# Tying normalised rows and turned residual blocks behind the next block's weight split in a hybrid attention layer

## The chip, the cores and the metric

The kernel runs on one core of one Trainium2 chip, in one launch. The metric is the device time in microseconds of that core, as the median of several runs: 1050.98 us here (three runs, 1050.15 to 1051.49). The core has five engines that each work through a queue of their own in order: TensorE (PE for its matmuls, PEld for the weight loads that go ahead of them), VectorE (DVE), ScalarE (ACT), GpSimd (POOL) and SyncE (SP, which here only issues DMAs). An instruction that waits for a semaphore holds up everything behind it in its engine's queue.

## The reference, cut to what matters

One post-norm decoder layer: 256 tokens and 16 meta tokens of width 2048, all in float32.

```python
p = h @ w_in                                  # q heads, shared latent, indexer, pool channels
# group A: an indexer scores the keys, each query keeps its top 64, attention over the latent
# group B: trailing means over 2, 4, 8, 16 tokens minus the token, a map per group
mix = concat(A, B) @ w_o
h = layer_norm(ALPHA * h + mix, ln1_g, ln1_b)
z = causal_conv3(h @ w_up)                    # to 2 * 5632 channels
a, g = split(z)
f = (gelu(a) * g) @ w_down
h = layer_norm(ALPHA * h + f, ln2_g, ln2_b)
return h[:, N_META:]
```

The indexer's score of a key is `sum_h w[t,h] * relu(q_idx[t,h] . k_idx[s])`. The two layer norms need a mean and a variance over the 2048 channels of a token.

## The kernel before, in words

**Number format.** A float32 product is made from three matmuls of a reduced format. Every operand is split into an upper part, rounded by an ACT copy, and a lower part, which is what DVE has left after subtracting the upper part. For weights this is `fetch` (L109 to L125): one DMA of a 128x2048 block into a `wraw` buffer (L110), then for each half of the block an ACT copy (L123) and a DVE subtraction (L124) into `whl`. `product` (L189 to L197) runs three matmuls for each of the 16 tiles of the contraction: upper by upper (L195), upper by lower (L196), lower by upper (L197). So one block of weights with 258 columns of activations is 48 matmuls, and its first L197 needs the DVE half of the first split.

**Order of weights.** All weight blocks stand in one list, `stream`. `weights` (L161) hands out the next block and first calls `emit` for the blocks up to two ahead. There are three `wraw` and three `whl` buffers. `state["use"]` is the number of the next block that will be handed out, and `split[i]` keeps the last ACT and the last DVE instruction of block i's split.

**Order of instructions.** The kernel is traced in program order, and a scheduler then orders each engine's queue by what it reckons to be ready first, so an instruction can be issued much earlier than it is written, or later. `behind(i)` (L168) lays down an order: whatever is traced inside it is queued, if it runs on ACT, after the last ACT instruction of block i's split, and if it runs on DVE, after the last DVE instruction of it. It adds no wait for completion, and it leaves PE, POOL and SP alone. Before the change only `forms` is traced inside it.

**The stages.** In order of time: indexer queries (8 blocks) with `dots` (L346, scores of two indexer heads on PE, relus on ACT, sums on DVE), the `w_uk` block whose eight products are copied by ACT to `kt` (L395), with the dots of the last query block traced after the copy of h == 2; values, top-64 selection on DVE, query heads, attention and pooling; the output projection (16 blocks, `output`), which also makes sums and sums of squares over the channels on POOL (L629 to L633); then the feed-forward part (88 up blocks, `up f half`, with w_down blocks between them from f = 8 on).

**Around the change.** The first four pairs of up blocks (f < 4, eight blocks, FOLDED = 4) run on activations that are not normalised yet (`folded`). Their results are corrected afterwards by `unfold` (L712 to L720: DVE copy L715, DVE multiply L717, ACT L719, POOL add L720), followed by the convolution `conv` (ACT L707, DVE L708 and L709) and `gate` (ACT L724, DVE L725). The column sums over the channels that the first layer norm needs, `deviation` (L662, matmuls of a column of ones in `column_sums`, L242) and `deviation_rows` (L677), are traced inside the first of these blocks, after its tiles 7 and 14. While these eight blocks run, `normalise(m)` prepares the 16 normalised activations for f >= 4: POOL multiply (L689), DVE add (L690), ACT scale and shift (L691), ACT upper part (L693), DVE lower part (L694); three of them are traced behind each block until all 16 are made. After the pairs f = 4 and f = 5 eight DVE transposes each (L870) turn the 32x32 squares of the normalised rows in place, and from f = 6 to f = 11 `residual` (L701) moves them with 32 DMAs on ACT's queue into `y2`, the sum that the w_down products are added to. Every one of these DMAs reads all 16 turned tiles. PSUM is two pools of four banks: `big()` for the weight products, `small()` for the rest, `kt` and `dots` among it.

Of the kernel before, what the change touches and what calls it, by code (L numbers as in the profile page):

```python
# [17 lines left out]
P = 128  # L18
D = 2048
NM = 16  # L20
# [4 lines left out]
KT = D // P  # L25
# [11 lines left out]
FOLDED = 4  # L37
MF = 80 + C
NE = NQ + 2
# [28 lines left out]
def tile_layer(ctx, tc, xt, w_first, w_proj, w_uk, w_uv, w_pool, w_o, w_up, w_down, cols, rows, rel_bias, onehot, out):  # L68
    nc = tc.nc
# [7 lines left out]
    def big():  # L77
        return pm.tile([P, 512], F32, tag="mm", name="mm")

    def small():  # L80
        return pa.tile([P, 512], F32, tag="at", name="at")
# [4 lines left out]
    ps = small()  # L86
# [20 lines left out]
    state = {"next": 0, "use": 0}  # L107
# [53 lines left out]
    def weights(ahead=2):  # L161
        i = state["use"]
        state["use"] += 1
        prefetch(i + 1 + ahead)
        return ready.pop(i)

    @contextmanager
    def behind(i):  # L168

        upper, lower = (getattr(ins, "ins", ins) for ins in split[i])  # L170
        with tc.issue_after(upper), tc.issue_after(lower):
            yield
# [8 lines left out]
    def row_sums(i, hl):  # L181

        total = sb.tile([P, 1], F32, name=f"total{i}")
        nc.scalar.activation(raws[i], raws[i], AF.Copy, accum_out=total)
        hi, lo = (hl[-1][:, p, 256:] if isinstance(hl, list) else hl[:, p, 2048:] for p in range(2))
        nc.scalar.activation(hi, total.to_broadcast([P, 2]), AF.Copy)
        nc.vector.tensor_tensor(lo, total.to_broadcast([P, 2]), hi.bitcast(F32), op=ALU.subtract)

    def product(ps, hl, m, act, lo, hi, ks=range(KT), width=P, k0=0, k1=KT):  # L189

        for n in range(k0, k1):
            k = ks[n]
            wh, wl = hl[:, 0, k * width:k * width + m], hl[:, 1, k * width:k * width + m]
            ah, al = act[k][:, 0, lo:hi], act[k][:, 1, lo:hi]
            nc.tensor.matmul(ps, wh, ah, start=n == 0, stop=False)  # L195
            nc.tensor.matmul(ps, wh, al, start=False, stop=False)  # L196
            nc.tensor.matmul(ps, wl, ah, start=False, stop=n == KT - 1)  # L197
# [6 lines left out]
    for k0, k1 in [(k, k + 1) for k in range(9)] + [(9, 12), (12, 15), (15, 16)]:  # L204
# [6 lines left out]
        if k0 % 6 == 0:  # L211
            hl = wp.tile([P, 2, 2048 + 2], F32R, tag="whl", name="whl")
# [22 lines left out]
    def col(base, j):  # L235
        return cv[:, base + j:base + j + 1]
# [25 lines left out]
    ps = heads[0][0]  # L262
# [22 lines left out]
    for j in range(2):  # L285
        ps = heads[1 + j][0]
# [5 lines left out]
    ps = small()  # L292
# [53 lines left out]
    def dots(j, qi, pa_, heads):  # L346

        for i in heads:
            h = 2 * j + i
            pb = small()  # L350
            for o, n, t in ((pa_[:, S * i:S * i + S], S, slice(0, P)), (pb[:, :T], T, slice(P, S))):
                nc.tensor.matmul(o, qi[:, i, t], kidx[:, 0, :n], start=True, stop=False)
                nc.tensor.matmul(o, qi[:, i, t], kidx[:, 1 + i, :n], start=False, stop=True)
            rl = temp([P, KW], "rl")
            nc.scalar.activation(rl[:, :KA], pa_[:, S * i:S * i + KA], AF.Relu)
            nc.scalar.activation(rl[:, KA:], pb[:, :T], AF.Relu)
            for i2, (a, b) in enumerate(((0, KA), (KA, KW))):
                nc.vector.scalar_tensor_tensor(score[:, a:b], rl[:, a:b], widx[:, i2, h:h + 1], score[:, a:b],
                                               op0=ALU.mult, op1=ALU.add)
# [3 lines left out]
    for j in range(8):  # L363
        hl = weights()
        ps = big()
# [22 lines left out]
    for h in range(H):  # L388
        ps = small()
        for c in range(2):  # L390
            w = slice(1024 * c + h * HD, 1024 * c + h * HD + HD)
            nc.tensor.matmul(ps[:, :T], uk[:, 0, w], ctp[:, c, 0, :], start=c == 0, stop=False)
            nc.tensor.matmul(ps[:, :T], uk[:, 0, w], ctp[:, c, 1, :], start=False, stop=False)
            nc.tensor.matmul(ps[:, :T], uk[:, 1, w], ctp[:, c, 0, :], start=False, stop=c == 1)
        nc.scalar.activation(kt[:, h, :], ps[:, :T], AF.Copy)  # L395
        if h == 2:
            dots(7, qis[7], small(), (0, 1))

    y = sb.tile([P, KT, T], F32, tag="y", name="x", padded_shape=[P, KT, T])
# [3 lines left out]
    for i, (a, b) in enumerate(((0, NM), (NM, NM + P), (NM + P, T))):  # L403
# [6 lines left out]
        for g in range(2):  # L410
            ps = small()
# [27 lines left out]
    for h in range(H):  # L439
        hl = weights()  # L440
        ps = big()
# [5 lines left out]
    ps = small()  # L447
# [120 lines left out]
    for h in range(H):  # L568
# [3 lines left out]
        hl = weights()  # L572
        ps = big()
# [46 lines left out]
    folded = []  # L620
# [22 lines left out]
    for m in range(1, KT):  # L643
# [5 lines left out]
        if m == KC:  # L649
            ps = small()  # L650
# [34 lines left out]
    h_parts = []  # L685

    def normalise(m):
        yd = y[:, m, Q0:]
        nc.gpsimd.tensor_tensor(yd, yd, rs, op=ALU.mult)  # L689
        nc.vector.tensor_tensor(yd, yd, m2, op=ALU.add)  # L690
        nc.scalar.activation(yd, yd, AF.Identity, bias=col(LN1, 2 * m + 1), scale=col(LN1, 2 * m))  # L691
        a = ring.tile([P, 2, T], F32R, tag="act", name="hp")
        nc.scalar.activation(a[:, 0, :NQ], yd, AF.Copy)  # L693
        nc.vector.tensor_tensor(a[:, 1, :NQ], yd, a[:, 0, :NQ].bitcast(F32), op=ALU.subtract)  # L694
        h_parts.append(a)
# [108 lines left out]
    for item in plan:  # L804
        if item[0] in "AB":
            seven(*item)
            continue
        if item[0] == "down":
            _, part, c, g = item
            hl = weights()  # L810
            if c == 1:
                emit((last, spare)[g])
                if g == 0:
                    row_sums(last, ready[last])
            if g == 0:
                downs = [big(), big()]
            n = PARTS[part]
            for k in range(4 * g, 4 * g + 4):
                w = slice(512 * (k - 4 * g), 512 * (k - 4 * g) + 512)
                for i in range(2):  # L820
                    a, r = pairs[part][k // 2][f"a{i + 1}{k % 2 + 1}"]
                    nc.tensor.matmul(downs[i], a[:, 0, r], hl[:, 0, w], start=k == 0, stop=False)
                    nc.tensor.matmul(downs[i], a[:, 0, r], hl[:, 1, w], start=False, stop=False)
                    nc.tensor.matmul(downs[i], a[:, 1, r], hl[:, 0, w], start=False, stop=k == n - 1)
            if g == n // 4 - 1:
                for i in range(2):
                    yc = y2[:, i, 512 * c:512 * c + 512]
                    nc.vector.tensor_tensor(yc, yc, downs[i], op=ALU.add)
            continue
        _, f, half_ = item  # L830
        part = next(p for p in range(len(PARTS)) if f < sum(PARTS[:p + 1]))
        if half_ == 0:
            if f % 2 == 0:
                pair = fp.tile([P, 2, S], F32, name="za", tag="z0", bufs=3)
            both = []
        hl = weights()
        ps = big()
        if todo and f > FOLDED + half_:
            p, r = todo.pop(0)
            with behind(state["use"]):  # L840
                pairs[p].append(forms(r, len(pairs[p]), p == FAST))
        if f < FOLDED:
            k = 0
            if f + half_ == 0:
                product(ps[:, :NE], hl, P, folded, 0, NE, k1=7)
                deviation()
                product(ps[:, :NE], hl, P, folded, 0, NE, k0=7, k1=14)
                deviation_rows()
                k = 14
            product(ps[:, :NE], hl, P, folded, 0, NE, k0=k)  # L850
            while len(h_parts) < min(KT, 3 * (2 * f + half_ + 1)):
                normalise(len(h_parts))
            both.append(ps)
            if half_ == 0:
                continue
            both = [conv(i * FT + f, i, unfold(both[i]), pair[:, f % 2]) for i in range(2)]
        else:
            product(ps[:, :NQ], hl, P, h_parts, 0, NQ)
            both.append(conv(half_ * FT + f, half_, ps, pair[:, f % 2]))
            if half_ == 0:  # L860
                continue
        gate(*both)
        if part > FAST:
            a = fp.tile([P, 2, NE], F32R, name="gp", tag="gp", bufs=16)
            gated.append(two_parts(a[:, :, :S], both[0]))
        elif f % 2:
            todo.append((part, pair))
        if f in (FOLDED, FOLDED + 1):
            for m in range(8 * (f - FOLDED), 8 * (f - FOLDED) + 8):
                nc.vector.transpose(y[:, m, NM:], y[:, m, NM:])  # L870
        if FOLDED + 2 <= f < FOLDED + 8:
            for _ in range((6, 5, 5)[f % 3]):
                residual(*moves.pop(0))
# [57 lines left out]
    for i in range(2):  # L931
        t, mv = slice(i * P, (i + 1) * P), mvs[i]
        waiting = []
        for q, (a, b) in enumerate(cuts[i]):
            ps = small() if i else big()
# [91 lines left out]
```

## Time and profile before

| what | value |
|---|---|
| time, median of 3 runs | 1050.98 us (1050.15 to 1051.49) |
| profiled execution, its own time | 1050.0 us |
| span of that execution (first to last instruction) | 1048.2 us |
| mean granted TensorE clock | 0.998 |
| PE busy / PEld busy | 99% / 94% of the span |
| DVE busy | 85%, 890.0 us |
| ACT busy | 59%, 621.3 us |
| POOL busy | 20%, 212.4 us |
| HBM read | 232.50 MB, 224 GB/s over the span |

Busy shares are over the whole span. A matmul's recorded duration is longer than the distance to the next one (they are pipelined), so short losses of PE show in the distance between starts, not in its busy share. In a view of waits, a line names the engine and line that waited, the engine and line that ended the wait, the total in us, the number of waits and the longest.

### The profile page before, as it was taken

How to read it: one execution, taken by the hardware profiler on the slowest of the kernel's cores; microseconds unless marked ns; L12 is line 12 of the kernel's file. 1: busy time of each engine (PE TensorE's matmuls, PEld its weight loads, DVE VectorE, ACT ScalarE, POOL GpSimd, SP SyncE). 2: the span in 40 equal slices, each digit the busy share in tenths (PEclk: the TensorE clock that was granted, in tenths of full speed). 3: DMA queues.
4: the chain of work that ended last, by engine and by line, in shares of the span. 5: the costliest groups of instructions: out<-in, count | busy, mean ns of one | idle time of the engine just before them, and what ended most of it. 6: DMA issues, size and time to landing. Idle time of an engine off the chain costs nothing. (4 is left out here: it accounts for less than half of the span.)

```text
span 1048.2 us, 19242 instructions
## 1 busy us (share of the span) xinstructions
PE 1035.8 (99%) x7671; PEld 986.4 (94%) x7671; DVE 890.0 (85%) x1381; ACT 621.3 (59%) x998; POOL 212.4 (20%) x264
## 2 busy tenths in 40 slices
PE   9999999999999999999999999999999999999996
PEld 8998999999999999999999999999999999999985
DVE  6879468858879997898989989898898899989876
ACT  7566346745447765566556655566655666555674
POOL 1100014125436231102112011120211212220030
PEclk9999999999999999999999999999999999999999
DMA  8756542454552577898887787887878778787773
GB/s 324 256 172 241 185 153 97 143 194 162 197 191 92 198 228 226 274 297 275 270 289 277 277 279 267 286 275 266 285 271 288 273 284 275 266 285 270 290 224 128
DMA packets 59322, 249.75 MB, mean 238 GB/s; under 512 B 21686, under 2 KB 22112, under 8 KB 32224
## 3 DMA queue, kind: packets, MB, share of 16 engines
q1 hardware_dynamic: 34160, 229.76, 60.3%
q0 software_dynamic: 7600, 15.62, 7.8%
q10 hardware_dynamic: 17472, 3.15, 1.7%
q8 instruction: 60, 0.98, 0.4%
q14 instruction: 30, 0.25, 0.1%
HBM read 232.50 MB, written 2.11 MB: 224 GB/s over the span
## 5 line engine op out<-in xcount | busy, mean ns | idle before, releaser
L124 DVE TENSOR_TENSOR whl<-wraw,whl 128x1024 fp32r<-128x1024 f32 (+1 forms) x416 | 489.5, 1212 | 43.3 <-ACT whl L123 42.6
L123 ACT ACTIVATE whl<-wraw 128x1024 fp32r<-128x1024 f32 (+1 forms) x416 | 402.5, 1015 | 114.8 <-DVE wraw L119 28.5
L196 PE MATMUL mm<-hp,whl 128*128 128x258 f32 x1280 | 362.4, 283 | 0.0
L195 PE MATMUL mm<-hp,whl 128*128 128x258 f32 x1280 | 361.9, 283 | 0.0
L197 PE MATMUL mm<-hp,whl 128*128 128x258 f32 x1280 | 361.0, 282 | 0.0
L195 PEld LDWEIGHTS mm<-hp,whl 128*128 128x128 f32 x1280 | 242.4, 189 | 3.2
L196 PEld LDWEIGHTS mm<-hp,whl 128*128 128x128 f32 x1280 | 242.5, 189 | 3.1
L197 PEld LDWEIGHTS mm<-hp,whl 128*128 128x128 f32 x1280 | 242.9, 190 | 0.0
L195 PE MATMUL mm<-xp,whl 128*128 128x256 f32 (+5 forms) x384 | 111.8, 291 | 0.0
L196 PE MATMUL mm<-xp,whl 128*128 128x256 f32 (+5 forms) x384 | 108.9, 284 | 0.0
L197 PE MATMUL mm<-xp,whl 128*128 128x256 f32 (+5 forms) x384 | 108.7, 283 | 0.0
L707 ACT ACTIVATE z<-mm,cv 128x256 f32<-128x256 f32 x40 | 22.6, 565 | 93.9 <-PE mm L197 93.5
L196 PEld LDWEIGHTS mm<-xp,whl 128*128 128x128 f32 x384 | 72.3, 188 | 0.8 <-issue 0.5
L195 PEld LDWEIGHTS mm<-xp,whl 128*128 128x128 f32 x384 | 72.4, 189 | 0.6
L197 PEld LDWEIGHTS mm<-xp,whl 128*128 128x128 f32 x384 | 72.4, 189 | 0.3 <-DVE whl L124 0.2
L773 PE MATMUL at<-whl,gp 128*128 128x512 f32 x180 | 71.2, 395 | 0.0
L774 PE MATMUL at<-whl,gp 128*128 128x512 f32 x180 | 71.1, 395 | 0.0
L772 PE MATMUL at<-whl,gp 128*128 128x512 f32 x180 | 71.1, 395 | 0.0
L747 POOL TENSOR_TENSOR forms<-za 128x128 f32<-128x128 f32 x20 | 24.8, 1239 | 220.6 <-DVE za L725 214.9
L707 ACT ACTIVATE za<-mm,cv 128x256 f32<-128x256 f32 x40 | 22.6, 565 | 62.5 <-PE mm L197 61.7
L744 POOL TENSOR_TENSOR forms<-za 128x128 f32<-128x128 f32 x20 | 22.2, 1112 | 121.3 <-DVE za L725 117.2
L115 DVE TENSOR_TENSOR wraw<-wraw 128x512 f32<-128x512 f32 x36 | 24.7, 685 | 19.8 <-DMA wraw<-in_w_down 19.8
(327 smaller groups left out, 1950.1 us busy)
## 6 DMA issues: line engine op xcount, KB each, us to landing
wraw<-in_w_up SPq DMA_DIRECT2D x88, 1024.0 KB, 5.1
wraw<-in_w_down SPq DMA_DIRECT2D x80, 1024.0 KB, 6.2
wraw<-in_w_proj SPq DMA_DIRECT2D x24, 1024.0 KB, 5.0
wraw<-in_w_o SPq DMA_DIRECT2D x16, 1024.0 KB, 4.9
y<-v POOLq DMA_DIRECT2D x27, 256.0 KB, 8.7
y<-u POOLq DMA_DIRECT2D x18, 256.0 KB, 4.7
wraw<-in_w_first SPq DMA_DIRECT2D x8, 304.0 KB, 5.2
x<-in_xt SPq DMA_DIRECT2D x1, 2176.0 KB, 8.6
```

What stands on the lines that cost most here:

```text
L115: nc.vector.tensor_tensor(b12, b12, b11, op=ALU.subtract)
L123: upper = nc.scalar.activation(hl[:, 0, c], raw[:, c], AF.Copy)
L124: lower = nc.vector.tensor_tensor(hl[:, 1, c], raw[:, c], hl[:, 0, c].bitcast(F32), op=ALU.subtract)
L195: nc.tensor.matmul(ps, wh, ah, start=n == 0, stop=False)
L196: nc.tensor.matmul(ps, wh, al, start=False, stop=False)
L197: nc.tensor.matmul(ps, wl, ah, start=False, stop=n == KT - 1)
L707: nc.scalar.activation(z, src[:, 2:NQ], AF.Identity, bias=col(C_B, j), scale=col(C_W, 3 * j + 2))
L744: nc.gpsimd.tensor_tensor(s[:, 0], a21, a22, op=ALU.add)
L747: nc.gpsimd.tensor_tensor(s[:, 3], a11, a21, op=ALU.subtract)
L772: nc.tensor.matmul(ps, a[:, 0, i], hl[:, 0, w], start=j == 0, stop=False)
L773: nc.tensor.matmul(ps, a[:, 0, i], hl[:, 1, w], start=False, stop=False)
L774: nc.tensor.matmul(ps, a[:, 1, i], hl[:, 0, w], start=False, stop=j == n - 1)
```

## The change

Four edits.

1. The dots of the last query block are traced after the `kt` copy of h == 3, not of h == 2.
2. In the first up block, `deviation` comes after 8 tiles, not 7, and `deviation_rows` after 15, not 14.
3. `normalise` is traced inside `behind(state["use"])`: its ACT and DVE instructions are queued after the split of the block that is handed out next. Its POOL multiply is not tied.
4. The transposes are traced after the pairs f = 3 and f = 4, not 4 and 5, and inside `behind(state["use"])`.

```diff
         nc.scalar.activation(kt[:, h, :], ps[:, :T], AF.Copy)
-        if h == 2:
+        if h == 3:
             dots(7, qis[7], small(), (0, 1))
...
             if f + half_ == 0:
-                product(ps[:, :NE], hl, P, folded, 0, NE, k1=7)
+                product(ps[:, :NE], hl, P, folded, 0, NE, k1=8)
                 deviation()
-                product(ps[:, :NE], hl, P, folded, 0, NE, k0=7, k1=14)
+                product(ps[:, :NE], hl, P, folded, 0, NE, k0=8, k1=15)
                 deviation_rows()
-                k = 14
+                k = 15
             product(ps[:, :NE], hl, P, folded, 0, NE, k0=k)
-            while len(h_parts) < min(KT, 3 * (2 * f + half_ + 1)):
-                normalise(len(h_parts))
+            with behind(state["use"]):
+                while len(h_parts) < min(KT, 3 * (2 * f + half_ + 1)):
+                    normalise(len(h_parts))
...
-        if f in (FOLDED, FOLDED + 1):
-            for m in range(8 * (f - FOLDED), 8 * (f - FOLDED) + 8):
-                nc.vector.transpose(y[:, m, NM:], y[:, m, NM:])
+        if FOLDED - 1 <= f <= FOLDED:
+            with behind(state["use"]):
+                for m in range(8 * (f - FOLDED + 1), 8 * (f - FOLDED + 1) + 8):
+                    nc.vector.transpose(y[:, m, NM:], y[:, m, NM:])
```

## The prediction

> **What bounds the kernel now.** I read the busy shares first, then the waits of the weight loads, then busy time by stretch, and last the timelines around each wait.
>
> ```profile
> span 1048.2 us, 19242 instructions
> PE 1035.8 (99%) x7671; PEld 986.4 (94%) x7671; DVE 890.0 (85%) x1381; ACT 621.3 (59%) x998; POOL 212.4 (20%) x264
> ```
> ```profile
> PEld at L554 <- ACT df L546: 1.1, 1, 1.1
> PEld mm L197 <- DVE whl L124: 1.1, 3, 0.6
> ...
> PEld at L242 <- POOL sums L633: 0.4, 1, 0.4
> PEld at L352 <- ACT kt L395: 0.4, 1, 0.4
> ```
> ```profile
> 316.00:330.00 14.00, 14.00 (x120) 14.00 (x119) 14.00 (x22) 9.05 (x18) 13.28 (x15) 1.00 0.21 76
> ...
> 350.00:360.00 10.00, 9.93 (x83) 9.72 (x82) 10.00 (x19) 8.04 (x13) 2.71 (x2) 1.00 0.57 190
> 400.00:600.00 200.00, 200.00 (x1432) 188.88 (x1431) 178.71 (x246) 117.80 (x165) 30.88 (x36) 1.00 0.83 275
> ```
>
> The columns of the last fence are stretch, length, and busy us of PE, PEld, DVE, ACT and POOL, then granted clock, DMA share and GB/s. TensorE sets the end: it is busy 99% of the span, and in 400 to 600 us it never idles. So a change that adds no matmul can gain only what TensorE waits for. Of its waits, three lines of four are touched by the four edits: L352 (dots), L242 (column sums), L197 behind the splits. Beside these waits stands DVE, full in both the earlier stretches (14.00 of 14, 10.00 of 10): there the order of its queue decides which block's split comes late.
>
> **The change part by part.** A matmul of 258 or 260 columns follows the one before after 0.12 us, as 338.75 and 338.87 do in the second fence below; what a wait costs is the distance beyond that.
>
> *Dots.* PE first, then ACT.
> ```profile
> 81.69 0.28 PE L196 MATMUL mm<-xp,whl 128*128 128x258 f32 x1
> 81.99 0.39 PE L197 MATMUL mm<-xp,whl 128*128 128x258 f32 x1
> 82.22 0.28 PE L195 MATMUL mm<-xp,whl 128*128 128x258 f32 x1
> 82.64 0.39 PE L352 MATMUL at<-kidx,qi 128*128 128x272 f32 x1
> ...
> 81.11 1.06 ACT L123 ACTIVATE whl<-wraw 128x1024 fp32r<-128x1024 f32 x1
> 82.19 0.97 ACT L395 ACTIVATE kt<-at 128x272 f32<-128x272 f32 x3
> ```
> PE loses 0.18 us to 81.99, 0.11 us to 82.22 and 0.30 us to 82.64: 0.59 us. The second dots bank is the one that kt 0 leaves, and ACT copies it only after a split, at 82.19. One more kt product (six matmuls, 0.75 us) now goes ahead, but then all four banks are taken by kt, so the first dots bank too waits for the first copy, near 82.59. PE would get there at 81.34 + 0.75 = 82.09 and wait 0.5 us, unless the scheduler fills in query matmuls as at 81.69. Gain 0.59 at best, loss 0.1 at worst (a restart like 82.22's); I take 0.3, as both rows of filler and of copy lie near. Moved with it are 8 matmuls, 4 relus and 4 DVE sums, no DMA; the top-64 search behind them starts up to 0.75 us later, which the eight query blocks on PE (48 matmuls of 0.12 us each, 46 us) hide; without that cover it would cost the same 0.75 us.
>
> *Column sums.*
> ```profile
> 309.71 0.86 PE L242 MATMUL at<-ones,sums 128*128 128x64 f32 x6 [0.24 <-POOL sums L633]
> L633 POOL TENSOR_TENSOR sums<-sums,sq x1: 1627/1627/1627, 308.0 to 308.0; 128x258 f32<-128x258 f32 x1
> ```
> The squares are ready at 308.03 + 1.63 = 309.66. One more tile is three matmuls, 0.36 us, longer than the idle 0.24 us, so the wait goes, and perhaps the 0.11 us restart: 0 to 0.35, I take 0.3. Twelve matmuls of `deviation_rows` move by the same tile; they were not waiting. No queue of DMAs is passed.
>
> *Ties.* Two up blocks waited, PE first, then DVE, then ACT:
> ```profile
> 338.75 0.28 PE L195 MATMUL mm<-fold,whl 128*128 128x260 f32 x1
> 338.87 0.28 PE L196 MATMUL mm<-fold,whl 128*128 128x260 f32 x1
> 339.55 0.39 PE L197 MATMUL mm<-fold,whl 128*128 128x260 f32 x1 [0.40 <-DVE whl L124]
> 339.77 0.28 PE L195 MATMUL mm<-fold,whl 128*128 128x260 f32 x1
> ...
> 351.05 0.28 PE L196 MATMUL mm<-fold,whl 128*128 128x260 f32 x1
> 351.40 0.39 PE L197 MATMUL mm<-fold,whl 128*128 128x260 f32 x1
> ```
> ```profile
> 336.25 0.75 DVE L690 TENSOR_TENSOR x<-x,of_token 128x258 f32<-128x258 f32 x2
> ...
> 337.60 0.75 DVE L690 TENSOR_TENSOR x<-x,of_token 128x258 f32<-128x258 f32 x2
> 338.28 2.35 DVE L124 TENSOR_TENSOR whl<-wraw,whl 128x1024 fp32r<-128x1024 f32 x2
> ...
> 343.37 1.18 DVE L124 TENSOR_TENSOR whl<-wraw,whl 128x1024 fp32r<-128x1024 f32 x1
> ...
> 349.81 0.43 DVE L870 STREAM_TRANSPOSE x<-x 128x256 f32<-128x256 f32 x1
> 350.16 2.32 DVE L124 TENSOR_TENSOR whl<-wraw,whl 128x1024 fp32r<-128x1024 f32 x2
> 352.40 0.98 DVE L694 TENSOR_TENSOR hp<-x,hp 128x258 fp32r<-128x258 f32 x1
> ```
> ```profile
> 337.00 2.00 ACT L123 ACTIVATE whl<-wraw 128x1024 fp32r<-128x1024 f32 x2
> 348.42 2.00 ACT L123 ACTIVATE whl<-wraw 128x1024 fp32r<-128x1024 f32 x2
> ```
> The first wait costs 339.55 - 338.87 - 0.12 = 0.56 and a restart of 0.10, together 0.66 us; the second 0.35 - 0.12 = 0.23 and as much restart, 0.33 us. Counting the L690 from their first, the four at 336.25 and 337.60 are rows 12 to 15. Traced behind block up-2-0 (f = 2, first half) and the one after it, they are now tied behind the split at 338.28 or the next: 1.5 us leave the front of it. But ACT writes its first half only at 337.00 + 1.05 = 338.05, and what stands before that on ACT are rows 6 to 8, tied to a split long done. So DVE can start 338.28 - 338.05 = 0.23 us earlier and no more: gain 0.23, bounds 0 and 0.66. At the second wait ACT is done at 349.47 and DVE starts at 350.16, behind a transpose that is now tied behind a split after it.
> ```profile
> L870 DVE STREAM_TRANSPOSE x<-x x16: 396/431/436, 341.6 to 367.2; 128x256 f32<-128x256 f32 x16
> ```
> Five transposes from 341.6 to 349.81, some 0.35 us of DVE each (349.81 to 350.16), leave; the four L690 (1.5 us) come in. The 0.35 us in front of the split goes, and with the 0.23 from above the start is 349.5 to 349.6, the end 0.6 us earlier; 0.23 is needed. Gain 0.33, bounds 0 and 0.33.
>
> What is late next? Everything moved is wanted late: the last L694 ends at 353.4, and the first block that reads it begins three blocks (144 matmuls, 17.3 us) before 374.30, at 357.0, and needs its sixteenth tile 45 matmuls on, at 362.4, so 9 us cover the rows; if they used that up, each us more would be a us of PE. The transposes feed only the 32 DMAs on ACT's queue.
>
> **The sum.** 0.3 + 0.3 + 0.23 + 0.33 = 1.16 us off the profiled execution, 1050.0 (a span of 1048.2 and 1.8 us around it): 1048.8. The median lies 0.98 above that run, so 1049.8. All bounds at their best: 0.59 + 0.35 + 0.66 + 0.33 = 1.93 us, 1049.0; all at their worst, 0.1 slower, 1051.1.
>
> **The rivals.**
>
> *The ties don't bind.* On ACT no L691 or L693 stood in front of the split it is now tied behind, and the splits' ACT halves set their time. If the DVE order hardly changes, both block waits stay and only 0.6 us is gained: 1050.4. For it speaks the 0.23 us above; against it the five DVE items in front of the splits.
>
> *ACT's queue stops at the residual DMAs: slower.*
> ```profile
> 367.20 0.43 DVE L870 STREAM_TRANSPOSE x<-x 128x256 f32<-128x256 f32 x1
> 367.56 1.41 DVE L124 TENSOR_TENSOR whl<-wraw,whl 128x1024 fp32r<-128x1024 f32 x1
> ...
> 367.92 1.40 ACTq L701 DMA_DIRECT2D y<-x  x2
> 369.84 2.01 ACT L123 ACTIVATE whl<-wraw 128x1024 fp32r<-128x1024 f32 x2
> ...
> 371.60 2.35 DVE L124 TENSOR_TENSOR whl<-wraw,whl 128x1024 fp32r<-128x1024 f32 x2
> 374.30 0.28 PE L195 MATMUL mm<-hp,whl 128*128 128x258 f32 x1
> ```
> Before, the first DMA is issued 0.3 us after the last transpose. Transposes 8 to 15 now stand behind the split that ends at 368.97. Between that and the next split at 371.60 lie 2.6 us of other DVE work; with half of it and eight transposes of 0.35 us, the last ends at 368.97 + 1.3 + 2.8 = 373.1 and not 367.6, and an L701 that keeps its place holds ACT 5.5 us longer. Behind it on ACT is the split of the block that PE begins at 374.30; its DVE half is done at 371.60 + 1.2 = 372.8, needed two matmuls in, at 374.54, and has 1.7 us to spare. So PE loses 3.8 us, net 2.6 slower: 1053.6. It decides from a last transpose after 367.6 + 1.7 = 369.3. Against it: DVE, rid of the early transposes, reaches that split sooner, and the scheduler can put the DMAs further back, as what they move is wanted only many blocks later.
>
> *Contention moves the wait to the next block.*
> ```profile
> L690 DVE TENSOR_TENSOR x<-x,of_token x16: 415/460/965, 315.5 to 337.9; 128x258 f32<-128x258 f32 x16
> ```
> An L690 follows the next after 0.37 us at 336.25, but takes up to 0.965 beside POOL's multiplies. The four moved ones now meet two POOL adds of `unfold` before the split at 343.37: 1.5 + 2 x 0.6 - 1.05 (three transposes gone) = 1.65 us later, where the next block, which PE begins 45 matmuls after 339.77, at 345.16, has its split at 344.55 and wants it at 345.40, 0.85 us to spare: 0.8 us back, 1050.6. The Trainium skill (SBUF — State Buffer, Who interferes with whom) says that a DVE instruction with two SBUF inputs and a GpSimd instruction that reads SBUF exclude one another, whichever starts first; the spread of L690 agrees. By that rule the transposes, with one input, cost POOL nothing.
>
> *More than the touched waits.* A new order from the dots on also removes the L554 wait of 1.1 us, with all of the 1.93: 3.0 us, 1048.0. Only the scheduler's freedom speaks for it.
>
> **How the numbers follow.** Forecast 0.50, ties idle 0.10, contention 0.08, ACT's queue 0.14, more 0.18. Of the forecast's own spread, 1049.0 to 1050.6, a median of three that scatters by 0.7 us takes a tenth beyond 2.1 us; 0.2%, 2.1 us, is about what a measurement of this kernel can tell from no change. Faster: 0.18 and 0.06 of the forecast, 0.24. Slower: 0.14 and 0.02, 0.16. Same: 0.60. The range goes from 1048.2, near the case of more, to 1052.4, halfway into the case of ACT's queue (a stall of 2.5 us); the forecast alone gives 1049.0 to 1050.6.
>
> **What would show it.** PE's wait at L242 gone; at L352 smaller; L197's total of 1.1 us down to some 0.4; L690 12 to 15 after the split near 338; no L870 before 355; the last L870 near 369 to 372. A PE wait near 374 with ACT held at L701 would prove the slower case; PE waits in stretches that have none now would make the forecast wrong altogether.

## The result, and the profile after

| what | before | after |
|---|---|---|
| time, median of 6 runs each | 1050.61 us (1049.91 to 1051.49) | 1055.04 us (1052.90 to 1057.46) |
| ratio to before | | 1.004, 95% interval 1.003 to 1.005 |
| profiled execution, its own time | 1050.0 us | 1057.46 us |
| its span | 1048.2 us | 1055.7 us |

The change makes the kernel 4.4 us slower; 1049.8 was forecast. The profiled execution of after is the slowest of its six runs, 2.4 us over the median, so its sizes are upper ones. The head of its page and its waits of the weight loads:

```profile
span 1055.7 us, 19243 instructions
PE 1037.3 (98%) x7671; PEld 987.4 (94%) x7671; DVE 889.9 (84%) x1381; ACT 621.0 (59%) x998; POOL 211.9 (20%) x264
```
```profile
PEld at L773 <- DVE whl L124: 5.4, 1, 5.4
...
PEld at L554 <- ACT df L546: 1.1, 1, 1.1
...
PEld at L352 <- ACT kt L395: 0.6, 1, 0.6
```

The busy shares hardly differ from before, DVE's work is the same 890 us, and ACT's is 621. The list of waits differs: L242 behind the column sums is gone, and so is L197 behind the splits, all 1.1 us of it. In their place stands one wait, 5.4 us, at a line (L773, a product of the w_down blocks) that did not wait at all before. To see where it lies, the start of the same matmul in both traces (numbers count the core's 7671 matmuls from 0):

| matmul | before, us | after, us | after - before |
|---|---|---|---|
| 2600 | 327.12 | 326.88 | -0.24 |
| 2700 | 339.77 | 338.87 | -0.90 |
| 3000 | 376.10 | 375.04 | -1.06 |
| 3600 | 455.59 | 454.52 | -1.07 |
| 4000 | 512.08 | 518.68 | +6.60 |
| 7300 | 974.42 | 981.01 | +6.59 |
| 7670 (the last) | 1038.58 | 1045.55 | +6.97 |

So of the forecast gain of 1.16 us nearly all arrived, 1.06 us by 376 us, and was kept for 80 us. Then 7.7 us were lost in one place between 455 and 519 us, and kept to the end. Of the other 0.9 us of the span, 0.4 lie between 981 us and the last matmul and 0.5 behind it; no edit touches these. The place itself, in after's timelines of PE, DVE and SP:

```profile
457.78 0.40 PE L772 MATMUL at<-whl,right 128*128 128x512 f32 x1
463.28 0.79 PE L773 MATMUL at<-whl,right 128*128 128x512 f32 x1 [5.11 <-DVE whl L124]
463.88 0.63 PE L774 MATMUL at<-whl,right 128*128 128x512 f32 x1
```
```profile
452.60 0.69 DVE L118 TENSOR_TENSOR wraw<-wraw 128x512 f32<-128x512 f32 x1 [0.74 <-DMA wraw<-in_w_down]
...
455.70 0.43 DVE L725 TENSOR_TENSOR za<-za,z 128x256 f32<-128x256 f32 x1
461.40 0.69 DVE L118 TENSOR_TENSOR wraw<-wraw 128x512 f32<-128x512 f32 x1 [5.28 <-DMA wraw<-in_w_down]
462.01 4.09 DVE L124 TENSOR_TENSOR whl<-wraw,whl 128x1024 fp32r<-128x1024 f32 x4
```
```profile
449.62 0.33 SPq L110 DMA_DIRECT2D wraw<-in_w_up  x1
451.89 0.33 SPq L110 DMA_DIRECT2D wraw<-in_w_down  x1
```

Three weight blocks matter. By their place in `stream` they are numbers 71 (w_down), 72 (up) and 73 (w_down). A w_down block of this kind is first folded in its `wraw` buffer by three DVE instructions (L118 to L120 of `fetch`) and then split as any block is (L123 on ACT, L124 on DVE); another kind has one such instruction, L115. The row at 452.60 is the fold of block 71. PE begins block 71 at 457.78 and needs its lower half for the second matmul. DVE had nothing to do from 456.1 on, but the next row in its queue was the fold of block 73, whose transfer was issued only at 451.89 and landed at 461.4, 9.5 us later. The four L124 behind it are the lower halves of blocks 71 and 72. ACT had made the upper halves of block 71 by 455.97, so its split was ready during the whole wait; those of block 72, whose transfer landed at 458.0, were made by 460.1. Before, at the same place, the order was the other one:

```profile
454.14 0.69 DVE L120 TENSOR_TENSOR wraw<-wraw 128x512 f32<-128x512 f32 x1
...
455.66 1.22 DVE L124 TENSOR_TENSOR whl<-wraw,whl 128x1024 fp32r<-128x1024 f32 x1
456.79 0.42 DVE L725 TENSOR_TENSOR za<-za,z 128x256 f32<-128x256 f32 x1
457.13 3.22 DVE L124 TENSOR_TENSOR whl<-wraw,whl 128x512 fp32r<-128x512 f32 x3
460.28 0.68 DVE L118 TENSOR_TENSOR wraw<-wraw 128x512 f32<-128x512 f32 x1
```

There the splits of 71 and 72 stand ahead of the fold of 73, which comes at 460.28 and waits for nothing. So the loss was a row of DVE's queue that waits for a DMA ahead of rows that are ready. The Trainium skill (TensorE: Matmul & The Clock Gate, Architectural detail) calls the queues of ACT and DVE strict first-in, first-out; the 5.28 us in which DVE idled with block 71's split ready behind the fold agree.

What led up to it shows in the groups of the transposes and of the residual DMAs, after (L872 is L870 of before):

```profile
L872 DVE STREAM_TRANSPOSE x<-x x16: 397/430/439, 357.0 to 374.7; 128x256 f32<-128x256 f32 x16
```
```profile
L701 ACTq DMA_DIRECT2D y<-x x32: 592/602/3017, 375.2 to 474.1; - x32
```

The figures are shortest, median and longest ns, then first and last start. Before, the transposes ran from 341.6 to 367.2 and the DMAs were issued from 367.9 to 464.0:

```profile
L701 ACTq DMA_DIRECT2D y<-x x32: 592/626/1987, 367.9 to 464.0; - x32
```

The tie has put the last transpose 7.5 us later and the first DMA 7.3 us. Of the 10.1 us by which the last DMA is later, most is not a cause of the loss but its result: in the run e2 below, which keeps all ties and has no stall near 460, the last DMA is issued at 466.4, 2.4 us later than before.

### The profile page after: what moved, and what is told of

The parts are those of the page before. It is cut to its first block, busy times and chain, and to the rows that moved or that the text cites. A ratio compares the mean times of both kernels' runs of the same rounds, so it can differ in the third digit from the quotient of the medians.

```text
span 1055.7 us, 19243 instructions
## 1 busy us (share of the span) xinstructions
PE 1037.3 (98%) x7671; PEld 987.4 (94%) x7671; DVE 889.9 (84%) x1381; ACT 621.0 (59%) x998; POOL 211.9 (20%) x264
## 5 line engine op out<-in xcount | busy, mean ns | idle before, releaser
L124 DVE TENSOR_TENSOR whl<-wraw,whl 128x1024 fp32r<-128x1024 f32 (+1 forms) x416 | 489.7, 1212 | 46.3 <-ACT whl L123 45.5
L123 ACT ACTIVATE whl<-wraw 128x1024 fp32r<-128x1024 f32 (+1 forms) x416 | 402.9, 1015 | 133.2 <-DVE wraw L119 32.3
L197 PE MATMUL mm<-hp,whl 128*128 128x258 f32 x1280 | 361.3, 282 | 0.0
L197 PEld LDWEIGHTS mm<-hp,whl 128*128 128x128 f32 x1280 | 243.1, 190 | 0.0
L197 PE MATMUL mm<-xp,whl 128*128 128x256 f32 (+5 forms) x384 | 108.6, 283 | 0.0
L197 PEld LDWEIGHTS mm<-xp,whl 128*128 128x128 f32 x384 | 72.4, 189 | 0.0
L773 PE MATMUL at<-whl,gp 128*128 128x512 f32 x180 | 71.4, 397 | 0.0
L115 DVE TENSOR_TENSOR wraw<-wraw 128x512 f32<-128x512 f32 x36 | 24.7, 686 | 20.4 <-DMA wraw<-in_w_down 20.4
```

Source lines behind the costliest of these rows:

```text
L115: nc.vector.tensor_tensor(b12, b12, b11, op=ALU.subtract)
L123: upper = nc.scalar.activation(hl[:, 0, c], raw[:, c], AF.Copy)
L124: lower = nc.vector.tensor_tensor(hl[:, 1, c], raw[:, c], hl[:, 0, c].bitcast(F32), op=ALU.subtract)
L773: nc.tensor.matmul(ps, a[:, 0, i], hl[:, 1, w], start=False, stop=False)
```

## The experiments

Theory A: the loss is the order on DVE alone, the fold of block 73 ahead of the splits of 71 and 72; the tie of the transposes (edit 4) makes this order, and the other edits are harmless. Rival R1: the residual DMAs, which now come later on ACT's queue, cost the time by themselves, by holding ACT or by slowing the weight transfers. Rival R2: the earlier start of everything behind 339 us, or the tie of the normalised rows, is to blame. Line numbers in the traces of the experiments differ by a few where lines were put in.

**e1: the changed kernel, transposes traced where edit 4 puts them, but not tied.**

```diff
         if FOLDED - 1 <= f <= FOLDED:
-            with behind(state["use"]):
+            if True:
                 for m in range(8 * (f - FOLDED + 1), 8 * (f - FOLDED + 1) + 8):
```

> The changed kernel with the transposes traced after f = 3 and 4 but not tied behind a split; the other edits kept. Theory (the tie on the transposes alone pushes the residual DMAs back on ACT, and with them the order of splits on DVE near 460 us): the 5.3 us wait of the w_down block on L124 is gone, as is the slow clock behind it, and the gains near 310, 340 and 351 stay: 1049.2 to 1050.0, against about 1050.6 before. Rival (the tie on the normalised rows moves the DVE backlog into the w_down blocks): the wait near 460 stays, 1054 to 1057.

Measured: 1050.84 us, median of 10 runs, beside 1050.85 of 25 runs of before; ratio 0.9999, interval 0.9990 to 1.0009. The loss is gone, but the time is above the expected 1049.2 to 1050.0, as most of the gain is gone too:

```profile
PEld mm L197 <- DVE whl L124: 1.0, 2, 0.6
```
```profile
337.62 0.43 DVE L872 STREAM_TRANSPOSE x<-x 128x256 f32<-128x256 f32 x1
337.98 2.31 DVE L124 TENSOR_TENSOR whl<-wraw,whl 128x1024 fp32r<-128x1024 f32 x2
```

Both waits of the splits near 339 and 351 are back, though the normalised rows are still tied: untied transposes take the place that these rows left in front of the split. The gain near 339 needs both ties, as e3 below has the transposes' tie alone and does not have it; the loss needs the tie of the transposes.

**e2: the changed kernel with the fold of block 73 queued behind the lower split of block 71.**

```diff
-    def fetch(raw, hl, src, kind=None):
+    def fetch(raw, hl, src, kind=None, after=None):
...
         if kind == "B":
-
-            nc.vector.tensor_tensor(b12, b22, b12, op=ALU.subtract)
-            nc.vector.tensor_tensor(b11, b12, b11, op=ALU.add)
-            nc.vector.tensor_tensor(b21, b21, b11, op=ALU.subtract)
+            with ExitStack() as tied:
+                if after is not None:
+                    tied.enter_context(tc.issue_after(after))
+                nc.vector.tensor_tensor(b12, b22, b12, op=ALU.subtract)
+                nc.vector.tensor_tensor(b11, b12, b11, op=ALU.add)
+                nc.vector.tensor_tensor(b21, b21, b11, op=ALU.subtract)
...
-        split[i] = fetch(raw, hl, stream[i], kinds.get(i))
+        after = getattr(split[71][1], "ins", split[71][1]) if i == 73 else None
+        split[i] = fetch(raw, hl, stream[i], kinds.get(i), after)
```

> The changed kernel with one DVE subtraction (L118 of w_down block B 0 0 3) queued behind the lower split of block B 0 0 2; nothing else in any queue moves. Theory A (the stall is the order on DVE: an L118 that waits for its own weight transfer stands ahead of a split whose data are there): PE's wait falls from 5.3 us to under 0.8, time 1049.0 to 1050.5, and the spread of runs shrinks. Theory B (the weight transfers themselves are late, held up by the residual DMAs, and PE must wait for them in any order): the wait stays above 3 us, only moved, 1053 to 1056.

Measured: 1050.74 us (10 runs), ratio 0.9997, interval 0.9988 to 1.0007. That is 0.2 us above the expected range, and no faster than before by what these runs can tell. The profiled execution, 1049.51 us and the fastest of the ten, has a span of 1047.7 us. The order of DVE's queue differs from the changed kernel's in one row, the first L118 of block 73. Its DVE timeline (L127 is the lower split, L121 the first fold):

```profile
453.93 4.36 DVE L127 TENSOR_TENSOR whl<-wraw,whl 128x1024 fp32r<-128x1024 f32 x4
458.65 0.69 DVE L121 TENSOR_TENSOR wraw<-wraw 128x512 f32<-128x512 f32 x1 [0.36 <-DMA wraw<-in_w_down]
```
```profile
L705 ACTq DMA_DIRECT2D y<-x x32: 592/593/1043, 374.6 to 466.4; - x32
```

DVE still waits for the transfer of block 73, 0.36 us, but with nothing ready behind it, and PE starts the block's second matmul 0.23 us after the first, as it does without a wait. A wait behind an ACT split that costs PE 0.5 us at 477.0 is all that is left of the loss in the stretch. This is theory A's test: one row moved gives back the whole loss, while transposes and residual DMAs (L705 here) keep the places that the change gave them. R1 as the cause of the loss near 460 falls, and so does R2, for everything else is kept.

**e3: before with edit 4 alone.** The edit is the last hunk of the change and nothing else.

> Only the edit of the transposes (tied, traced after f = 3 and 4). Theory: the whole loss and none of the gain at the column sums, little of that at the splits: 1054.5 to 1057, a PE wait of 4 to 6 us on L124 near 460. Rival (the loss needs the tied rows too): within 1 us of before.

Measured: 1055.65 us (4 runs), ratio 1.0048, interval 1.0033 to 1.0063: the whole loss, by the tied transposes alone. The waits of its profiled execution:

```profile
PEld at L773 <- DVE whl L124: 3.3, 1, 3.3
PEld at L772 <- DVE y L780: 1.8, 1, 1.8
```
```profile
481.23 0.69 DVE L780 SCALAR_TENSOR_TENSOR y<-y,v 128x512 f32<-128x512 f32 x1 [3.69 <-DMA y<-x]
```

The first is the same inversion; the wait, 3.2 us by the starts of the matmuls, is shorter than the 4 to 6 us expected. The second is new: L780 adds a w_down product into `y2` and stands in DVE's queue until the residual DMAs that fill it have landed. So R1 has a share of its own in this execution, the longest of the four, 1.8 us of PE at 482 us, by late residual DMAs that stop DVE, not ACT. In the changed kernel L780 waits for them too, 1.3 us, and PE loses nothing by it. Of the early gains e3 has one: near 339 PE loses 0.67 us as before, near 351 nothing, where before it lost 0.34. So the gain near 351 can be had from the tie of the transposes alone.

**e4: before with edits 1 and 2 alone** (dots and column sums, the first two hunks).

> Only the later dots and the later column sums. By the terms: column sums 0.3 us off, dots between 0 and 0.6 (the changed kernel showed a wait of 0.55 us there, so 0): 1050.1 to 1050.4 against 1050.6, both split waits near 339 and 351 as before.

Measured: 1051.71 us (10 runs), ratio 1.0003, interval 0.9994 to 1.0013. In the trace the wait at L242 is gone, which gains 0.28 us by the starts of the matmuls; the dots gain 0.02 us. PE then comes earlier to the split near 351 and waits 0.43 us there in place of 0.23. The median was expected between 1050.1 and 1050.4 and missed that: 0.3 us is below what ten runs resolve, as the ten went from 1050.14 to 1052.64. In the profiled execution, 1051.66 us, matmul 7300 starts 0.04 us earlier than before; the 1.7 us by which its span is longer are all lost behind that matmul, where neither edit acts. These edits cost nothing that explains 4.4 us.

**e5: the changed kernel with the residual DMAs traced earlier**, 8, 7, 6, 5, 4 and 2 of them behind the six pairs in place of 6, 5, 5, 6, 5, 5. The aim was to undo the lateness that the tie brings.

```diff
-            for _ in range((6, 5, 5)[f % 3]):
+            for _ in range((8, 7, 6, 5, 4, 2)[f - FOLDED - 2]):
                 residual(*moves.pop(0))
```

> The changed kernel, all ties kept, with the 32 residual DMAs traced 8, 7, 6, 5, 4 and 2 behind f = 6 to 11 instead of 6, 5, 5, 6, 5, 5. In the resulting DVE queue no subtraction of block B 0 0 3 stands ahead of the split of B 0 0 2. Theory (the tie acts only through where the DMAs fall and the order that the scheduler then makes of the splits): no PE wait over 1 us near 460, 1049.3 to 1051. Rival (the tied transposes themselves, or DMAs beside the weight transfers, cost the time): 1053 to 1056.

Measured: 1055.28 us (4 runs), ratio 1.005, interval 1.0034 to 1.0066. The expectation of a time near before's failed: the rival's range, 1053 to 1056, is the one that holds, though not, as the rows show, for the rival's reason. Its waits, and its DVE at the two places:

```profile
PEld mm L197 <- DVE whl L124: 3.1, 1, 3.1
PEld at L773 <- DVE whl L124: 3.1, 1, 3.1
```
```profile
427.77 0.69 DVE L115 TENSOR_TENSOR wraw<-wraw 128x512 f32<-128x512 f32 x1 [7.27 <-DMA wraw<-in_w_down]
428.38 4.63 DVE L124 TENSOR_TENSOR whl<-wraw,whl 128x1024 fp32r<-128x1024 f32 x4
...
448.92 0.69 DVE L118 TENSOR_TENSOR wraw<-wraw 128x512 f32<-128x512 f32 x1 [2.14 <-DMA wraw<-in_w_down]
```

The inversion at block 73 is gone, but the moved DMAs led the scheduler to two others: the fold of one w_down block ahead of splits of blocks before it, at 427.77 and at 448.92. PE waits 2.8 us at 429.65 and 3.1 us at 451.53. In the stretch before the first of them ACT too was held, 5.04 us, by five residual DMAs:

```profile
417.61 5.04 ACTq L701 DMA_DIRECT2D y<-x  x5
422.75 3.90 ACT L123 ACTIVATE whl<-wraw 128x1024 fp32r<-128x1024 f32 x4 [4.58 <-issue]
```

Its splits were done at 426.65 all the same, before DVE's fold could start; whether the hold costs anything is what e8 shows.

**e6: the changed kernel with the residual DMAs traced 7, 7, 6, 6 and 6 behind five pairs.** In this queue order two folds stand ahead of ready splits, while the last DMA is issued at 462.9 us, 11 us earlier than in the changed kernel and 3.5 us earlier than in e2.

```diff
-        if FOLDED + 2 <= f < FOLDED + 8:
-            for _ in range((6, 5, 5)[f % 3]):
+        if FOLDED + 2 <= f < FOLDED + 7:
+            for _ in range((7, 7, 6, 6, 6)[f - FOLDED - 2]):
```

> The changed kernel with the residual DMAs traced 7, 7, 6, 6 and 6 behind f = 6 to 10. Now all three subtractions of block B 0 0 1 stand ahead of the split of B 0 0 0 on DVE, and all three of B 0 0 3 ahead of that of B 0 0 2. Theory (order on DVE): two PE waits on L124, some 2 us near 442 and 5 us or more near 460, each with a slower clock behind it: 1055 to 1062, slower than the changed kernel's 1055. Rival (late DMAs, not order): these DMAs end earlier than the changed kernel's, so it should be the faster one, 1051 to 1053.

Measured: 1060.75 us (4 runs, 1056.40 to 1062.49), ratio 1.0089, interval 1.0071 to 1.0106.

```profile
PEld at L773 <- DVE whl L124: 7.0, 3, 4.8
```
```profile
426.53 0.69 DVE L115 TENSOR_TENSOR wraw<-wraw 128x512 f32<-128x512 f32 x1 [6.54 <-DMA wraw<-in_w_down]
427.14 4.62 DVE L124 TENSOR_TENSOR whl<-wraw,whl 128x1024 fp32r<-128x1024 f32 x4
...
446.83 0.69 DVE L118 TENSOR_TENSOR wraw<-wraw 128x512 f32<-128x512 f32 x1 [4.22 <-DMA wraw<-in_w_down]
```

Earlier DMAs and twice the loss: it goes with the order, not with the lateness of the DMAs. The time is as expected, the places are not. PE loses 1.2 us at 428.41, 4.5 us at 450.17 and 0.4 us at 468.91, where some 2 us near 442 and 5 us near 460 were expected, and the first fold to wait is an L115, of the other kind of block.

**e7: the changed kernel with the folds L118 to L120 of every w_down block queued behind the lower split of the block before, and the dots back behind h == 2.** The edit is e2's with another condition:

```diff
-        after = getattr(split[71][1], "ins", split[71][1]) if i == 73 else None
+        after = getattr(split[i - 1][1], "ins", split[i - 1][1]) if kinds.get(i) == "B" else None
```

> A version meant to keep the gains alone: the changed kernel with the subtractions of every B block queued behind the split before it, and the last dots back behind h == 2. Theory: waits at the column sums, near 339 and near 351 gone, none near 460, that of the dots as before: 1049.4 to 1050.4, ratio 0.9985 to 0.9995 of before. Rival: 1050.8, if moved DMAs take back what the early stretch gains.

Measured: 1050.13 us, median of 12 runs, beside 1050.77 of 17 of before; ratio 1.0006, interval 0.9992 to 1.0021. The profiled execution has 1049.22 us and a span of 1047.4, with no wait at 339, 351 or 460. That execution is the fastest of the twelve, though, and two of them took 1054.71 and 1058.21 us; these have no profile. The median lies in the expected range, the ratio does not (0.9985 to 0.9995 expected), and no gain is shown.

**e8: e5 with the folds of both kinds of w_down block (L115 too) queued behind the lower split of the block before.** The condition becomes `kinds.get(i) in ("A", "B")`, and L115 stands in such an `ExitStack` as well.

> The kernel of e5 (residual DMAs traced 8, 7, 6, 5, 4, 2 to the block pairs, 1055.3 us) with one thing more: in every w_down block the folding subtractions (L115, L118 to L120 of the changed kernel) are queued on DVE behind the lower split of the block before. Theory A (what costs time is the order on DVE, a subtraction that waits for its own transfer ahead of a split that is ready): the waits of 2.8 and 3.1 us near 430 and 452 go and the time returns to 1049.5 to 1051.5. Rival (the residual DMAs on ACT's queue, now issued earlier, cost the time by holding ACT or by slowing the weight transfers): both stay as in e5, the time stays at 1054 to 1056, with PE waits near 430 and 452 behind ACT instead of DVE.

Measured: 1050.98 us (10 runs, 1048.88 to 1055.43) beside 1050.56 (21 runs); ratio 1.0005, interval 0.9996 to 1.0015. The residual DMAs stand as in e5, the loss of e5, 4.5 us against its own before, is gone: it too was the order. The execution that was profiled is the longest of the ten, 1055.43 us, and shows what the order can't mend. PE has no wait near 430, though ACT was held there for 5.8 us by the residual DMAs. PE loses 1.3 and 0.9 us at 453.7 and 455.0, where ACT starts a split at 452.62, 0.1 us after the block's transfer has landed, 10.5 us after its issue: there, in this execution, PE waits behind ACT as the rival had it. It loses 1.7 us more at 471.85 behind the sum into `y2` (L787, L780 before):

```profile
469.37 0.69 DVE L787 SCALAR_TENSOR_TENSOR y<-y,v 128x512 f32<-128x512 f32 x1 [4.04 <-DMA y<-x]
469.97 0.69 DVE L126 TENSOR_TENSOR wraw<-wraw 128x512 f32<-128x512 f32 x1
470.58 2.36 DVE L130 TENSOR_TENSOR whl<-wraw,whl 128x1024 fp32r<-128x1024 f32 x2
```

**e9: e7 with the folds of both kinds ordered**, the version meant to beat both kernels.

> The changed kernel with the dots back after h == 2 and the folding subtractions of both kinds of w_down block (L115, L118 to L120) queued behind the lower split of the block before; e7 had this for L118 to L120 alone. By the early gains alone (column sums 0.3, wait near 339 0.7, near 351 0.15) it should be 1.1 us below before, 1049.3 to 1050.2, and without a wait near 460. Rival: queueing every subtraction late makes some split late where the transfer came in time; then waits of PE behind L124 appear in 400 to 1000 us and the time is 1051 to 1054. Single runs of 1054 or more, as two of the twelve of e7, should be absent if they came from A blocks out of order; if they come again, the order of these blocks is not their cause.

Measured: 1049.78 us, median of 11 runs, beside 1050.56 of 21 of before; ratio 1.0000, interval 0.9988 to 1.0013. The profiled execution, the fastest of the eleven, has 1048.97 us and a span of 1047.2, and PE is busy throughout the stretch of the loss, at full clock (the columns are those of the prediction's table of stretches):

```profile
450.00:470.00 20.00, 20.00 (x143) 18.80 (x143) 17.56 (x25) 12.04 (x15) 2.87 (x3) 1.00 1.01 326
```

The typical run of e9 is 0.8 us below before, near the expected 1.1, but two runs of eleven took 1052.24 and 1056.61 us, so the ratio is 1.0000 and no gain is shown. As in e7 there are single long runs. The folds with L115 stand in order here, so their order is not the cause of these.

## Why the prediction was wrong

**The terms of the sum.** Together they were right: 1.16 us were forecast, and the four places gained 1.14 us. (Matmul 3000 shows 1.06, as this execution was 0.09 us behind at matmul 619 already, ahead of the first edit.) One by one they were less so, and that the sum fits is luck: two terms were too large, one was too small.

- *Dots: 0.3 forecast, 0.03 measured.* The lower case that I had worked out came: the four `kt` copies start at 82.27, PE waits for the first of them until 82.72, and no query matmuls fill in. From matmul 619 to 752 (79 to 100 us) the changed kernel gains 0.03 us.
- *Column sums: 0.3 forecast, 0.28 measured.* One more tile covers the idle time, and the wait is gone.
- *Split near 339: 0.23 forecast, 0.67 measured, the upper bound.* What was wrong in this term is the limit set by ACT ("ACT writes its first half only at 337.00 + 1.05", with rows 6 to 8 in front of it). ACT did not stay as it was. Its timeline, after:

```profile
331.79 0.60 ACT L707 ACTIVATE z<-u,cv 128x256 f32<-128x256 f32 x1 [0.31 <-POOL u L720]
332.41 1.28 ACT L724 ACT_TABLE_LOAD   x1
...
336.13 1.05 ACT L123 ACTIVATE whl<-wraw 128x1024 fp32r<-128x1024 f32 x1
```

  Before, an L691 stood ahead of the gate's table load, which came at 333.46. Without it and with the convolution earlier, the gate is 1.05 us and the split 0.87 us earlier, and DVE follows at 337.22 instead of 338.28.
- *Split near 351: 0.33 forecast, 0.16 measured.* Of the wait of 0.23 us 0.07 are left, and the restart of 0.10 us is still paid.

**The step that failed** is "What is late next?". There I followed the moved instructions to those who read them, found 9 us of cover for the rows, and settled the transposes with one sentence: they "feed only the 32 DMAs on ACT's queue". That is true, and e2 shows that in the changed kernel neither their lateness nor the DMAs' cost the time. What I left out is that a tie also changes what the scheduler puts first elsewhere. With the transposes and the DMAs behind them moved back, it chose 90 us further on another order for two w_down blocks: 73's fold ahead of 71's split, which cost 7.7 us in the profiled execution and 4.4 us net in the median. From the landing of 73 to the start of L773 it is 1.9 us (461.40 to 463.28), and PE wanted L773 at 458.0, so the transfer had to land by 456.1, 4.2 us after its issue; it took 9.5, and the fastest of that stretch take 4.8. My last sentence named the sign ("PE waits in stretches that have none now would make the forecast wrong altogether") but no rival had it as its mechanism, and no chance was given to it.

**The rivals.** *ACT's queue stops at the residual DMAs* had the right beginning and the wrong end. The last transpose starts at 374.7, later than the 369.3 from which I had it decide, and the DMAs wait for it. But PE has no wait near 374: the DMAs moved back behind the splits on ACT, as I had put against it. That it gave 1053.6, not far from the 1055.0, is chance. *The ties don't bind* is refuted by the 0.67 us, *contention* by PE's even run from 340 to 350, and *more than the touched waits* by L554, still 1.1 us.

**What stays open.** That edit 4 makes the inversion, and that the inversion makes the loss near 460, is shown (e3, e2). That the way from the one to the other leads over the place of the residual DMAs is made likely by e5 and e6, where moving only those moves the inversions; the scheduler's own reckoning stands in no trace. Edit 3 without any of edit 4 was not run. The single runs of 1052 to 1058 us in e7 and e9 have no profile. Three of the four recorded a mean clock of 0.994 or 0.995, the other runs of e7 and e9 0.996 to 0.998. By my estimate a clock lower by 0.003 over 1050 us is 6 us of half clock, as after a long wait of PE; where they waited stays open. The longest of e8, which has one, shows transfers of 10.5 and 12.05 us and a sum that waits for residual DMAs, so late landings are a candidate, no more.

## What to carry to other kernels

In an in-order queue, look at every instruction that waits for a DMA and ask what stands behind it: a fold of a later block ahead of a ready split of an earlier one lets the ready work wait until the transfer has landed (here 5.28 us of DVE and 5.27 us of PE). Where a scheduler orders the queues, an edit that ties or moves instructions can change orders 90 us away in code that it doesn't touch, so compare the queues of before and after over their whole length, not at the edit alone. If an order matters, write it down: one tie on the fold gave back all that the change had lost.

## What the runs showed of the hardware that was not expected

**A wait of PE costs more than its length.** The wait near 460 took 5.27 us by the starts of the matmuls (463.28 - 457.78 - 0.23), but 7.7 us were lost there. The rest is the clock. After's stretches, with the granted clock in the third column from the end:

```profile
458.00:461.50 3.50, 0.18 (x1) 0.00 (x0) 0.10 (x1) 2.45 (x3) 0.00 (x0) 1.00 0.75 163
461.50:468.30 6.80, 5.02 (x15) 4.24 (x16) 6.62 (x10) 1.12 (x2) 0.00 (x0) 0.50 0.52 186
468.30:478.00 9.70, 9.70 (x75) 9.30 (x74) 7.74 (x11) 6.45 (x9) 1.88 (x2) 1.00 0.98 323
```

The clock is halved 3.3 us after the end of PE's last matmul (457.78 + 0.40) and comes back 5.0 us after PE's restart. Meanwhile the 512-column matmuls follow one another after 0.43 us (six steps from 463.88 to 466.44) where they take 0.23 otherwise. With the other waits of about 3 us and more it is alike: 4.5 us of PE in e6 bring half clock too, for 6.8 us, 3.2 us in e3 and 3.1 us in e5 for 3.4 us, and 2.8 us in e5 bring none. But the length of one wait does not decide alone: in e8 the two waits of 1.3 and 0.9 us, both between 452.19 and 454.99, were followed by 3.4 us of half clock, from 454.83 on.

```profile
448.90:455.60 6.70, 5.43 (x19) 4.86 (x20) 6.70 (x11) 1.01 (x2) 0.00 (x0) 0.50 0.64 215
```
```profile
429.60:433.00 3.40, 3.35 (x19) 2.80 (x20) 3.40 (x4) 0.96 (x2) 0.00 (x0) 1.00 0.46 94
452.20:455.50 3.30, 3.30 (x17) 3.30 (x17) 3.30 (x9) 0.99 (x2) 0.00 (x0) 0.50 1.09 258
```

The first of these is e6's stretch from its longer wait on, the others are e5's after its two waits. So of two losses of like length one is paid once and the other by more than its length. The Trainium skill (TensorE: Matmul & The Clock Gate, What's actually happening) states half clock after one idle window of about 3.4 us; the lengths of 3.4 and 6.8 us are one and two such windows. But 3.1 and 3.2 us of waiting were enough here: a whole idle window of that length does not fit into them, so there the measurement and the rule as stated differ.

**Transfers of the same size land very unevenly.** The 1 MB weight blocks that SP issues between 375 and 500 us take 4.8 to 9.5 us to land in the changed kernel, 4.7 to 9.1 us before, and up to 12.05 us in e8's profiled execution. An order of the queue that holds only with a middling landing time is therefore not safe.
